# Issuing the 2 MB loads of a rotary-embedding and score kernel as two 1 MB loads each, in consecutive steps

## The chip, the cores and the metric

The kernel runs on one core of a Trainium2 chip. The metric is the device time of one execution, in microseconds, as the median of several; lower is better. A run is timed in turn with runs of the kernel before on the same chip. The trace of one execution of each kernel comes from the hardware profiler. A run counts as "slow", and is left out of ratios, when it is over 1.5% above the fastest of the same kernel.

## The reference

```python
batch, seq, heads, dim = 16, 512, 16, 64            # q, k: float32; cos, sin: [seq, dim / 2]
q1, q2 = q[..., :half_dim], q[..., half_dim:]
q_rot = np.concatenate([q1 * cos_q - q2 * sin_q, q1 * sin_q + q2 * cos_q], axis=-1)
# k_rot in the same way
scores = np.einsum('bshd,bthd->bsht', q_rot, k_rot)  # float32, 268 MB
```

Both inputs are 34 MB each and the output is 268 MB, so four fifths of the bytes are stores.

## The kernel before

The output is made in 64 steps, four for each batch b. A step rotates one quarter ("slot" c) of q and of a later k on DVE, transposes on PE, computes eight pairs of score matrices on PE, copies them from PSUM to a staging buffer on ACT, and stores 4 MB. There are three staging buffers, and two buffers each for q and k. Every transfer of the main loop is issued by SP on one queue, in program order, apart from the "relieved" q loads.

```python
RELIEVED = {("q", 5): 0, ("q", 8): 1, ("q", 11): 2, ("q", 14): 3}
...
def load(which, b):
    t = inb[which][b % 2]
    sem = f"in_{which}{b % 2}"
    rows = [("in", which, b % 2, c) for c in range(C)]
    rest = [("in rest", which, b % 2, c) for c in range(C)]
    if (which, b) not in RELIEVED:
        dma(SP, nc.sync, t.rearrange("p c (h d) -> p c h d", h=H), dram[which][b], sem, writes=rows + rest)
        return
    # relieved: 120 of the 128 partitions are loaded through POOL's queue. A cursor is first moved
    # so that the 15 shares leave out one of the 16 DMA engines (SLOW = 4).
    ...
    plan.add(POOL, None, (), rows)        # POOL waits until the buffer is free
    ...
    halves(0, n, rows, f"part{x}")
...
load("k", 3)
for i in range(C, NST):
    ...                                   # the step; its store is issued when ACT has filled the buffer
    if i % C == C - 2:
        load("q", i // C + 2)
    elif i % C == C - 1:
        load("k", i // C + 3)
```

An engine list ("plan") records what each operation reads and writes and derives every semaphore wait from it, so moving a load can't make a race.

## Time and profile before

| | |
|---|---|
| median of 3 runs | 798.94 us (797.91 to 799.68) |
| PE, ACT, DVE busy | 86%, 71%, 68% of the span |
| 16 DMA engines busy | 99% of the span, 421 GB/s on average |
| transfers | 18,513 packets, 335.87 MB |

The row to look at is the DMA's: every slice but the first and the last is at 9, and PE, busy as it is, waits for ACT, which waits for staging buffers. The lines follow in the prediction.

### The profile page before, as it was taken

The page shows a single profiled execution, that of the slowest core. Times are in us where ns is not written, and L with a number is a line of the kernel's source. Part 1 is how long each engine was busy: PE and PEld are TensorE (multiplying, and loading weights), DVE is VectorE, ACT ScalarE, POOL GpSimd, SP SyncE. Part 2 cuts the span into 40 slices and gives each one's busy share as a digit, 9 for nine tenths or more (in the row PEclk, how much of TensorE's full clock was granted, in tenths as well). Part 3 has the DMA queues.
Part 4 walks back from the last instruction along what each step waited for, and adds up shares of the span by engine and source line. Part 5 has one row for each costly group of instructions (what it writes and reads, how often), then busy time and mean ns, then how long its engine had stood idle before and what let it go on. Part 6 is the DMA issues. An engine that isn't in the chain of part 4 may idle for free.

```text
span 797.1 us, 8197 instructions
## 1 busy us (share of the span) xinstructions
PE 684.3 (86%) x3072; PEld 295.4 (37%) x3072; DVE 545.2 (68%) x516; ACT 562.4 (71%) x647; POOL 8.4 (1%) x18
## 2 busy tenths in 40 slices
PE   3989999897989979799797988979989699789960
PEld 2444443343333434344342433334334244334420
DVE  6999988575775868568585767757758488575400
ACT  3978886785767858578585866768667677678860
POOL 0000000000000000100000000000000100000000
PEclk9999999898998989989898999989989899899995
DMA  8999999999999999999999999999999999999995
GB/s 346 420 424 433 429 418 434 426 434 423 430 413 427 435 434 428 439 421 414 426 427 437 432 435 426 419 428 432 428 431 433 432 429 411 428 432 437 430 433 238
DMA packets 18513, 335.87 MB, mean 421 GB/s; under 512 B 2128, under 2 KB 3408, under 8 KB 4432
## 3 DMA queue, kind: packets, MB, share of 16 engines
q1 hardware_dynamic: 16832, 327.42, 96.5%
q0 software_dynamic: 1376, 8.13, 2.4%
q10 hardware_dynamic: 288, 0.13, 0.1%
q8 instruction: 6, 0.10, 0.0%
q14 instruction: 11, 0.09, 0.0%
HBM read 67.24 MB, written 268.44 MB: 421 GB/s over the span
## 4 chain that ended last, share of the span: by engine, by line
DMA 47%; PE 35%; DVE 8%; ACT 6%; issue 1%; ACTq 0%; DVEq 0%; SPq 0%
DMA out_dram<-st 47%; PE ps L409 27%; PE bank L360 9%; ACT st L418 6%; DVE st L335 3%; DVE part L335 2%; DVE k_sb L335 2%; DVE q_sb L335 1%; DMA st<-in_k_dram 1%; DVE kT L378 0%; DVE qT L378 0%; ACTq L110 0%; DVEq L110 0%; SPq L542 0%; SPq L513 0%
## 5 line engine op out<-in xcount | busy, mean ns | idle before, releaser
L418 ACT COPY st<-ps 128x1024 f32<-128x1024 f32 x512 | 495.5, 1018 | 196.7 <-DMA out_dram<-st 103.3
L409 PE MATMUL ps<-kT,qT 64*128 64x512 f32 x2048 | 542.9, 646 | 71.6 <-ACT st L418 71.6
L409 PEld LDWEIGHTS ps<-kT,qT 64*128 64x128 f32 x2048 | 182.0, 195 | 261.0 <-issue 134.2
L378 DVE COPY qT<-bank 128x512 f32<-128x512 f32 x118 | 81.6, 691 | 197.3 <-PE bank L360 197.3
L360 PEld LDWEIGHTS bank<-ident,q_sb 128*128 128x128 f32 x480 | 54.7, 150 | 101.5 <-issue 99.5
L360 PE MATMUL bank<-ident,q_sb 128*128 128x128 f32 x480 | 85.5, 305 | 1.0 <-DVE q_sb L335 1.0
L360 PEld LDWEIGHTS bank<-ident,k_sb 128*128 128x128 f32 x480 | 50.4, 141 | 94.5 <-DVE k_sb L335 43.1
L360 PE MATMUL bank<-ident,k_sb 128*128 128x128 f32 x480 | 78.6, 287 | 1.6 <-DVE k_sb L335 0.8
L378 ACT COPY kT<-bank 128x512 f32<-128x512 f32 x122 | 72.5, 597 | 6.7 <-PE bank L360 6.7
L335 DVE TENSOR_TENSOR part<-q_sb,ss_t 128x1024 f32<-128x1024 f32 x60 | 73.5, 1225 | 3.2
L335 DVE TENSOR_TENSOR k_sb<-k_sb,part 128x1024 f32<-128x1024 f32 x60 | 73.5, 1225 | 2.1
L335 DVE TENSOR_TENSOR k_sb<-k_sb,cos_t 128x1024 f32<-128x1024 f32 x60 | 73.5, 1225 | 2.0
L335 DVE TENSOR_TENSOR q_sb<-q_sb,cos_t 128x1024 f32<-128x1024 f32 x60 | 73.5, 1225 | 2.1
L335 DVE TENSOR_TENSOR part<-k_sb,ss_t 128x1024 f32<-128x1024 f32 x60 | 73.0, 1216 | 0.3
L335 DVE TENSOR_TENSOR q_sb<-q_sb,part 128x1024 f32<-128x1024 f32 x60 | 72.9, 1216 | 0.0
L360 PE MATMUL bank<-ident,st 128*128 128x128 f32 x64 | 10.8, 319 | 13.2 <-DVE st L335 13.2
L360 PEld LDWEIGHTS bank<-ident,st 128*128 128x128 f32 x64 | 8.2, 161 | 18.5 <-DVE st L335 16.7
L335 DVE TENSOR_TENSOR part<-st,ss_t 128x1024 f32<-128x1024 f32 x8 | 9.8, 1222 | 6.4 <-DMA st<-in_k_dram 6.0
L335 DVE TENSOR_TENSOR st<-st,part 128x512 f32<-128x512 f32 x16 | 11.1, 691 | 0.5
L237 POOL DMA_DIRECT2D scratch<-in_q_dram x6 | 3.6, 600 | 615.4 <-PE bank L360 615.4
L335 DVE TENSOR_TENSOR st<-st,cos_t 128x1024 f32<-128x1024 f32 x8 | 9.8, 1225 | 0.3
L378 ACT COPY qT<-bank 128x512 f32<-128x512 f32 x10 | 5.7, 615 | 3.5 <-PE bank L360 3.5
(11 smaller groups left out, 11.0 us busy)
## 6 DMA issues: line engine op xcount, KB each, us to landing
out_dram<-st SPq DMA_DIRECT2D x60, 4096.0 KB, 25.5
k_sb<-in_k_dram SPq DMA_DIRECT2D x15, 2048.0 KB, 27.1
q_sb<-in_q_dram SPq DMA_DIRECT2D x11, 2048.0 KB, 29.2
out_dram<-st SPq DMA_DIRECT2D x16, 1024.0 KB, 13.3
q_sb<-in_q_dram POOLq DMA_DIRECT2D x4, 1920.0 KB, 32.6
st<-in_k_dram SPq DMA_DIRECT2D x1, 1536.0 KB, 9.0
st<-in_q_dram SPq DMA_DIRECT2D x1, 1536.0 KB, 12.2
st<-in_k_dram SPq DMA_DIRECT2D x1, 512.0 KB, 5.0
```

The lines of the kernel that those rows point to most:

```text
L237: plan.add(engine, one(lambda: e.dma_start(dst, src)), reads, writes, sem=sem, also=also)
L335: plan.add(DVE, one(lambda: nc.vector.tensor_tensor(o, a, b, op=op)), reads, writes, also=more)
L360: done = [nc.tensor.transpose(bank[:, x, :], srcs[x], ident) for x in range(4)]
L378: plan.add(engine, one(lambda: copy(out=dst, in_=src)), [("bank", m)], keys)
L409: nc.tensor.matmul(out=ps[:, r, :], lhsT=lhs[lo:hi, :], rhs=rhs[lo:hi, :], start=True, stop=True)
L418: plan.add(ACT, one(lambda: nc.scalar.copy(out=so, in_=si)), [("ps", y)], [("st", s, p)])
```

## The change

Two 2 MB loads come after two of each four stores, and none after the other two. The change is meant to spread them, 1 MB behind each store, so that the queue always has the same mix.

```diff
-    def load(which, b):
+    def load(which, b, half=None):
...
         if (which, b) not in RELIEVED:
-            dma(SP, nc.sync, t.rearrange("p c (h d) -> p c h d", h=H), dram[which][b], sem, writes=rows + rest)
+            lo, hi = (0, C) if half is None else (half * C // 2, (half + 1) * C // 2)
+            dma(
+                SP, nc.sync, t[:, lo:hi].rearrange("p c (h d) -> p c h d", h=H), dram[which][b][:, lo:hi],
+                sem if half is None else f"{sem}_{half}", writes=rows[lo:hi] + rest[lo:hi],
+            )
             return
...
-    load("k", 3)
+    load("k", 3, 0)
...
-        if i % C == C - 2:
+        if i % C == 0:
+            load("k", i // C + 2, 1)
+        elif i % C == C - 1:
+            load("k", i // C + 3, 0)
+        elif ("q", i // C + 2) not in RELIEVED:
+            load("q", i // C + 2, i % C - 1)
+        elif i % C == C - 2:
             load("q", i // C + 2)
-        elif i % C == C - 1:
-            load("k", i // C + 3)
```

## The prediction

> **What bounds the kernel now.** I read the page's shares of busy time first, then the slices, then the queues, then the chain that ended last, and only then the waits.
>
> The page of the kernel before, busy shares, slices and queues (DMA is the mean busy share of the 16 DMA engines in tenths, GB/s what they moved):
> ```profile
> PE 684.3 (86%) x3072; PEld 295.4 (37%) x3072; DVE 545.2 (68%) x516; ACT 562.4 (71%) x647; POOL 8.4 (1%) x18
> ...
> DMA  8999999999999999999999999999999999999995
> GB/s 346 420 424 433 429 418 434 426 434 423 430 413 427 435 434 428 439 421 414 426 427 437 432 435 426 419 428 432 428 431 433 432 429 411 428 432 437 430 433 238
> DMA packets 18513, 335.87 MB, mean 421 GB/s; under 512 B 2128, under 2 KB 3408, under 8 KB 4432
> ...
> q1 hardware_dynamic: 16832, 327.42, 96.5%
> q0 software_dynamic: 1376, 8.13, 2.4%
> ```
> PE has the most busy time of the computing engines, 86%, and could be taken for the bound. The DMA row says otherwise: every slice is at 9, the first and last excepted, and the queues' shares add to 99%. The stretches of the timeline, split in four, say it with more digits (the columns are the stretch, its length, busy time of PE, PEld, DVE, ACT and POOL, granted clock, DMA share, GB/s):
> ```profile
> 20.00:200.00 180.00, 165.47 (x779) 73.22 (x779) 148.71 (x143) 140.19 (x165) 1.45 (x2) 0.96 1.01 428
> 200.00:400.00 200.00, 178.42 (x788) 75.93 (x786) 139.27 (x131) 143.19 (x164) 2.48 (x4) 0.92 1.00 426
> 400.00:600.00 200.00, 177.15 (x782) 75.02 (x780) 138.37 (x131) 141.53 (x163) 1.33 (x2) 0.93 1.00 429
> 600.00:780.00 180.00, 155.38 (x704) 66.28 (x700) 105.56 (x101) 131.27 (x149) 2.47 (x4) 0.94 1.01 430
> ```
> The DMA share is 1.00 in each. It can pass 1 because two queues interleave on one engine and both packets' times then count. I also counted, from the packet records, how many of the 16 engines have a packet open at each moment: between 15 us after the first packet and the last 10 us there is no 5 us stretch in which 3% of them are idle. There is no hole to fill.
>
> Each of the 64 steps has a 4 MB store (4.194 MB decimal) and on average a quarter of two 2 MB loads (1.049 MB): 5.243 MB, at 428 GB/s 12.25 us. PE needs 684.3/64 = 10.7 us a step and ACT 562.4/64 = 8.8 us. So the transfers set the pace, and 64 times 12.25 us is 784 us; the start and the last stores make the rest.
>
> The chain that ended last, the waits (total us, times, longest) and the issues (KB each, median us from issue to landing) agree:
> ```profile
> DMA 47%; PE 35%; DVE 8%; ACT 6%; issue 1%; ACTq 0%; DVEq 0%; SPq 0%
> ...
> ACT st L418 <- DMA out_dram<-st: 103.3, 30, 7.0
> ...
> SPq L237 <- ACT st L418: 714.1, 76, 16.9
> ...
> out_dram<-st SPq DMA_DIRECT2D x60, 4096.0 KB, 25.5
> k_sb<-in_k_dram SPq DMA_DIRECT2D x15, 2048.0 KB, 27.1
> q_sb<-in_q_dram SPq DMA_DIRECT2D x11, 2048.0 KB, 29.2
> ```
> ACT waits 103.3 us for a store to free a staging buffer: that is the transfers holding back the computing. No line of the waits has DVE waiting for k_sb or q_sb to land, so no load is late. A store lands 25.5 us after its issue though its own 4.194 MB take 9.8 us at 428 GB/s: about 15 us of work lies queued ahead of it. That backlog is why the lumps of two 2 MB loads in four steps leave no hole.
>
> **What the Trainium skill says.** "DMA: Bandwidth & Descriptors", section "Where 436 GB/s comes from", puts the ceiling of the 16 engines at 435 GB/s; the stretches' 426 to 430 are 98 to 99% of that, so the trace agrees that little is left. The same page, "Why small descriptors are slow", gives a fixed overhead of about 3 cycles a packet, so halving a large packet should cost nearly nothing; the packet records here put the fixed part at some 7 ns (below). The same page, "Anatomy of one DMA", fits about 2.0 us of fixed cost to each DMA of the software path, most of it waiting for the last write to be confirmed. This case's SP loads use the hardware path, and on the busy engines the trace shows no such hole between one transfer and the next: packets follow each other directly. And "Rules for kernel authors" asks for at least 1 MiB for each DMA at 128 partitions; the halves are just that.
>
> **The change part by part.**
>
> *What is moved.* k loads from batch 3 on and the q loads from batch 3 on that are not relieved through POOL are split by slot: 13 of k and 9 of q, 22 loads become 44. The order of instructions has 105 rows on SP before and 127 after, which confirms 22; PE, DVE, ACT and POOL have the same rows in the same order. The q half 0 goes one step earlier than the whole did and k half 1 one step later. A k slot of half 1 is first used five steps after its new issue, q half 1 six steps; at 12.25 us a step that is over 60 us against some 27 us to landing. Nothing becomes late.
>
> *What is removed.* No byte. ACT's 103.3 us of waiting will be spread differently, because every step now has 5.24 MB rather than steps of 4.19 and 6.29 MB. As the 16 engines have no hole, this smoothing has nothing to give: 0 us.
>
> *What is added.* A 2 MB load has 128 packets of 16 KB, 8 on each engine. Its two halves have 256 of 8 KB, 16 on each engine, and one more completion write on each. So each engine gets 22 x 8 = 176 packets and 22 completions more. The packet records of before give the medians: 32 KB 1213 ns (7,680 packets), 16 KB 611 ns (3,350), 8 KB 309 ns (3,057, of which 992 are loads of just such half rows through POOL, also 309), 4-byte completions 9 ns. That is linear in the size plus about 7 ns. Two 8 KB packets take 618 where one of 16 KB took 611: 7 ns more. But on one engine a packet starts 3 to 4 ns before the end of the one before, so the true step is 305 or 306 against 607, and the pair costs 3 to 5 ns more. I take both as bounds: 176 x 4 ns = 0.7 us to 176 x 7 ns = 1.2 us. Completions: 22 x (5 to 9 ns) = 0.1 to 0.2 us. **Sum: +0.8 to +1.4 us on each engine**, and because the engines never rest all of it lies on the path that sets the end. SP also issues 22 more transfers of about 1 us, inside the 714.1 us that it waits for ACT: 0 us.
>
> 798.94 + 1.1 = 800.0 us.
>
> **The rivals.**
>
> *Smoothing pays.* If ACT's 103.3 us of waits delayed stores until engines ran dry, even steps would bring some of it back. For it: the 30 waits, up to 7.0 us long. Against it: the DMA share of 1.00 in all four stretches, and the 15 us of backlog. At most it could give what separates 428 from 435 GB/s, 1.6% or 13 us; I expect none of it, as that difference is packets running at their own length.
>
> *Better or worse interleaving.* Some 16 KB packets are stretched: their mean is 635 against the median of 611 ns, in total 24 x 3,350 / 16 = 5.0 us an engine. Most of that is in the four k loads that run beside a relieved q load of POOL (3.2 us), where two queues share an engine and the stretched time is the other queue's data. Splitting moves which packets overlap, not how many bytes do. The remaining 1.8 us could go either way: +/- 1 us.
>
> *Halves cost more than their packets.* If each additional transfer left a hole of 2 us on the busy engines, 22 would add 44 us, to 843 us. Against it: completions here are followed by the next transfer's first packet without a gap. Or rows of 8 KB at a pitch of 16 KB in HBM might be read less evenly; against it, the 992 POOL packets of that shape at 309 ns.
>
> *The slowest engine sets the tail.* In the packet records fifteen engines end within 4.3 us of each other and one ends 3.5 us after the last of these; the relieved loads exist to help it, as one engine's 32 KB packets are mostly 20 to 50 ns longer. If a half load costs that engine more than others, a us or two; the end may also scatter so between executions, as the three times of before scatter over 1.8 us.
>
> **Range and chances.** 800.0 us from the sum. Below, the scatter of before (797.91 to 799.68) and a lucky interleaving allow 797.8; above, the scatter and the tail's engine allow 803.0. Two per cent is 16 us, more than the whole distance to the ceiling, so faster gets 0.01; slower needs the holes of the third rival: 0.02. I chose the middle of +0.8 and +1.4 rather than weighing the two bounds further.
>
> **What would show it.** The packets of the page should rise by 2,816 + 352 to 21,681 at the same 335.87 MB, the share of DMA stay at 1.00 in the stretches, and GB/s fall by less than 1. 8 KB packets should keep 309 ns. ACT's waits for stores should be more in number and shorter, with a similar total, about 100 us; no wait of DVE for q_sb or k_sb should appear. The prediction is wrong if a DMA slice falls below 9 in the middle, if 8 KB load packets take over 330 ns, or if the rate in the stretches passes 432 GB/s.

## The result

The changed kernel took **803.66 us** (four runs, 802.26 to 805.82) against 798.93 us of before. The ratio is 1.0062, with a 95% interval of 1.0037 to 1.0088. A ratio here and below is the mean time of one kernel's fast runs over that of the other's in the same rounds, so not quite the ratio of the medians. That is within 2%, as forecast, but it is 4.7 us, not 1.1 us, and lies above the range, which ended at 803.0.

The page after, slices and queues:
```profile
DMA  9999999999999999999999999999999999999997
GB/s 350 419 424 414 386 436 421 438 424 401 429 429 430 436 428 434 389 436 431 430 431 432 429 432 383 432 432 428 434 433 427 380 438 427 431 432 426 433 431 306
DMA packets 21682, 335.88 MB, mean 420 GB/s; under 512 B 2480, under 2 KB 3760, under 8 KB 4784
...
q1 hardware_dynamic: 20000, 327.43, 96.5%
q0 software_dynamic: 1376, 8.13, 2.8%
```
The packets are as counted ahead (21,681 forecast, 21,682 found). The DMA row is still all 9s but for its end. The GB/s row is not as before: five slices stand at 380 to 401, where before nothing in the middle was under 411. Busy engines moved fewer bytes. Also, q0, POOL's queue, takes 2.8% for the same 8.13 MB in place of 2.4%: its packets took longer.

The four stretches after, columns as in the prediction (the last two are DMA share and GB/s):
```profile
20.00:200.00 180.00, 168.02 (x794) 73.78 (x791) 151.70 (x145) 142.43 (x168) 1.45 (x2) 0.98 1.00 418
200.00:400.00 200.00, 172.16 (x776) 73.11 (x774) 138.59 (x130) 139.72 (x161) 2.48 (x4) 0.95 1.01 427
400.00:600.00 200.00, 177.45 (x782) 74.68 (x784) 137.93 (x130) 143.31 (x165) 1.33 (x2) 0.94 1.01 427
600.00:780.00 180.00, 155.96 (x700) 65.87 (x696) 104.66 (x100) 130.91 (x148) 2.48 (x4) 0.95 1.00 425
```
The first lost 10 GB/s against before, the third 2, the last 5. The waits and issues after:
```profile
ACT st L422 <- DMA out_dram<-st: 124.8, 39, 8.7
...
k_sb<-in_k_dram SPq DMA_DIRECT2D x26, 1024.0 KB, 28.6
q_sb<-in_q_dram SPq DMA_DIRECT2D x18, 1024.0 KB, 27.2
```
ACT's waits for stores were to become more and shorter at the same total. They became more (39 for 30), longer (8.7 us the longest) and larger in total (124.8 for 103.3 us).

**Where the time is.** Two places carry it. The first is the start of the main loop. SP's instructions after, in order of time (start, duration):
```profile
65.11 1.18 SPq L237 DMA_DIRECT2D k_sb<-in_k_dram  x1
76.21 0.33 SPq L237 DMA_DIRECT2D out_dram<-st  x1
```
The half of the first k load goes out at 65.11 us and the next store can only be issued at 76.21 us. A 2 MB load bridged that; a 1 MB load doesn't, and the engines ran dry: the DMA share in the first of the following stretches is 0.81, and by the packet records 1.15 us of all 16 engines went idle. The second place is the four POOL loads. Stretches of the changed kernel at the start and at each of these:
```profile
75.40:77.40 2.00, 2.00 (x14) 0.84 (x10) 1.93 (x3) 2.00 (x3) 0.00 (x0) 1.00 0.81 340
85.40:91.40 6.00, 6.00 (x32) 2.60 (x28) 5.70 (x7) 4.91 (x6) 0.00 (x0) 1.00 1.00 302
187.50:192.50 5.00, 3.20 (x17) 1.30 (x16) 2.01 (x3) 2.40 (x3) 0.00 (x0) 1.00 1.06 341
334.50:339.50 5.00, 3.46 (x18) 1.35 (x16) 2.75 (x3) 2.22 (x3) 0.00 (x0) 1.00 1.06 315
481.50:488.50 7.00, 3.99 (x16) 1.23 (x12) 2.48 (x3) 2.75 (x4) 0.00 (x0) 0.85 0.99 305
630.50:637.50 7.00, 3.38 (x16) 1.39 (x16) 1.92 (x3) 3.24 (x4) 0.00 (x0) 0.93 1.04 314
```
and those of the kernel before, at its start and its second and third POOL load:
```profile
85.40:91.40 6.00, 6.00 (x32) 2.63 (x29) 5.78 (x7) 4.91 (x6) 0.00 (x0) 1.00 0.99 426
...
333.50:338.50 5.00, 2.51 (x14) 0.76 (x10) 1.82 (x2) 0.56 (x2) 0.00 (x0) 1.00 0.99 419
481.50:488.50 7.00, 3.92 (x22) 1.53 (x18) 2.26 (x3) 2.80 (x4) 0.00 (x0) 1.00 1.01 431
```
With the DMA share at 0.99 or more in all but the first, the changed kernel moved 302 to 341 GB/s where the kernel before moved 419 to 431. (GB/s of so short a stretch is rough: the kernel before read 455 at its first POOL load.)

In the packet records it can be seen why the meeting is new. When POOL's load begins, it shares each engine with whatever SP's queue has there. Before, that was stores, and the two went on at 427 to 428 GB/s, averaged over each of the four loads. In the change the second half of the k load of the same batch, issued one step later than the whole load was, is still on its way then: 72, 93, 112 and 104 of its 128 packets were unfinished when the first POOL packet started (0 at all four before). Both loads' packets are stretched there; the 8 KB packets of POOL's queue have a mean of 352 ns in the whole run against 310 ns before, at a median of 309 ns in both.

For the comparisons below I worked out one measure from the packet records. At each moment the rates (bytes by duration) of all open packets are summed; what is missing to 432 GB/s, the rate of undisturbed stores, is lost time of the 16 engines together. "Start" is 67 to 97 us of the span, "POOL" the four POOL loads with 3 us ahead of and 2 us behind each, "behind" the 20 us after that, "rest" the remainder from 97 to 724 us. "Tail" is how long after the median engine the last engine ended its last store. Each row is one trace.

```
kernel                        start  POOL  behind  rest   sum   tail
before                          0.3   1.1    3.8   1.0    6.2    6.4
the change                      3.3   7.8    0.5   0.9   12.4    1.6
halves back to back (e1)        0.2   1.2    2.4   1.6    5.4    6.0
start half only (e12)           2.3   0.9    3.3   0.8    7.3    5.4
POOL halves only (e13)          0.3   2.2    1.9   1.3    5.7    5.6
start and POOL halves (e14)     2.6   7.1    0.2   0.5   10.4    3.0
relieved k whole (e2)           2.8   2.5    2.4   1.9    9.7    8.3
first k whole (e3)              0.3   1.9    5.2   4.7   12.1    7.9
both whole (e4)                 0.5   1.2    2.4   2.0    6.0    7.7
change, POOL waits (e17)        3.0   4.6    0.4   1.2    9.2    2.1
late whole k, no halves (e5)    0.3   3.0    1.3   0.8    5.3    4.2
```
The change lost 3.0 us more at the start and 6.7 us more beside the POOL loads, and 3.3 us less behind them, where the whole k loads of before are stretched: 6.2 us more in all. The packets add their own 1 us or so. Of these the time shows 3.4 us in the profiled runs (spans of 797.1 and 800.5 us), because the tail shrank by 4.8 us: in the kernel before, the last engine ended 6.4 us after the median one, so the median one had that much room. In the change the median engine's last store landed 8.2 us later (807.2 for 799.0 on the trace's clock), the last engine's only 3.3 us later (808.7 for 805.4).

Sum and tail together account for the profiled times: the span less both is 784.5 to 786.7 us in every row. So the table says of each trace whether its engines lost time together or one of them ended late. It doesn't say how either came about.

### The profile page after: what moved, and what is told of

The parts are those of the page before. It is cut to its first block, busy times and chain, and to the rows that moved or that the text cites. A ratio compares the mean times of both kernels' runs of the same rounds, so it can differ in the third digit from the quotient of the medians.

```text
span 800.5 us, 8241 instructions
## 1 busy us (share of the span) xinstructions
PE 680.5 (85%) x3072; PEld 292.0 (36%) x3072; DVE 545.2 (68%) x516; ACT 561.6 (70%) x647; POOL 8.4 (1%) x18
## 2 busy tenths in 40 slices
DMA packets 21682, 335.88 MB, mean 420 GB/s; under 512 B 2480, under 2 KB 3760, under 8 KB 4784
## 3 DMA queue, kind: packets, MB, share of 16 engines
q0 software_dynamic: 1376, 8.13, 2.8%
## 4 chain that ended last, share of the span: by engine, by line
DMA 52%; PE 31%; DVE 8%; ACT 5%; issue 1%; ACTq 0%; DVEq 0%; SPq 0%
DMA out_dram<-st 51%; PE ps L413 24%; PE bank L364 8%; ACT st L422 5%; DVE st L339 3%; DVE part L339 2%; DVE k_sb L339 2%; DVE q_sb L339 1%; DMA sin_t<-in_sin_dram 1%; DVE kT L382 0%; DVE qT L382 0%; ACTq L237 0%; ACT ss_t L459 0%; ACT ss_t L458 0%; ACTq L110 0%
## 5 line engine op out<-in xcount | busy, mean ns | idle before, releaser
L422 ACT COPY st<-ps 128x1024 f32<-128x1024 f32 x512 | 494.6, 1020 | 200.0 <-DMA out_dram<-st 124.8
L413 PEld LDWEIGHTS ps<-kT,qT 64*128 64x128 f32 x2048 | 179.3, 193 | 269.4 <-ACT st L422 139.1
```

The costliest lines, as they stand in the source:

```text
L413: nc.tensor.matmul(out=ps[:, r, :], lhsT=lhs[lo:hi, :], rhs=rhs[lo:hi, :], start=True, stop=True)
L422: plan.add(ACT, one(lambda: nc.scalar.copy(out=so, in_=si)), [("ps", y)], [("st", s, p)])
```

## The experiments

Each kernel was checked for races first, all gave correct results, and each was timed in five rounds (e6 and e7 in three) beside the kernel before on the same chip. The change itself was timed in a session of its own, so it is compared with an experiment through the two ratios to the kernel before.

**My first theory** was that the times of issue do the damage, at the start and at the POOL loads, and not the packets. The rival was the number and size of the transfers.

### e1: the halves, back to back

```diff
     load("k", 3, 0)
+    load("k", 3, 1)
...
-        if i % C == 0:
-            load("k", i // C + 2, 1)
-        elif i % C == C - 1:
+        if i % C == C - 1:
             load("k", i // C + 3, 0)
+            load("k", i // C + 3, 1)
...
+        elif i % C == C - 2 and ("q", i // C + 2) not in RELIEVED:
+            load("q", i // C + 2, 0)
+            load("q", i // C + 2, 1)
```

> The halves are kept (22 more transfers, 2,816 more 8 KB packets) but both halves of a load are issued one after the other at the step of the old whole load. Theory 1, the times of issue do the damage (a k half meets the POOL load of a relieved q, and the thin queue at the start): no collision, so +0 to +1.5 us against before, some 799 to 800.5 us. Rival, the smaller packets and the number of transfers cost it: as slow as the change, 803 to 805 us.

Measured: 800.03 us (798.78 to 801.08) against 798.74, ratio 1.0020 (1.0007 to 1.0033). So 22 transfers and 2,816 packets more cost 1.3 us by medians, 1.6 by the ratio. The rival falls. What sets the change apart from e1 is only the step of issue, and it is worth the difference of the ratios, 0.42% with an interval of some 0.13 to 0.71%: 3.4 us.

### e2, e3, e4: whole loads at the POOL loads, at the start, at both

e2 keeps the k loads of batches 5, 8, 11 and 14 whole at their old step, e3 the first k load, e4 both; everything else is as in the change.

```diff
-        if i % C == 0:
+        if i % C == 0 and ("q", i // C + 2) not in RELIEVED:          # e2
             load("k", i // C + 2, 1)
+        elif i % C == 0:
+            pass
         elif i % C == C - 1:
-            load("k", i // C + 3, 0)
+            load("k", i // C + 3, 0 if ("q", i // C + 3) not in RELIEVED else None)
```
```diff
-    load("k", 3, 0)
+    load("k", 3)                                                       # e3; step 4 then loads no k half
```

> The change, but the k loads of the four batches whose q is relieved (5, 8, 11, 14) stay whole at the old step, so no k half is in flight when a POOL load starts. The four collisions lost some 7.5 us in the trace of the change, and before lost 3.2 us at the whole k loads after each POOL load. Theory 1: 3 to 6 us faster than the change, 797.5 to 800.5 us, and no stretch under 400 GB/s at the POOL loads. Rival (packets and transfers): at most 0.5 us faster than the change, 803 us.

> The change, but the first k load of the main loop (batch 3) whole at its old place. In the trace of the change the engines ran dry for 1.15 us at the start of the main loop and the next half load ran at some 300 GB/s for 5 us, together 3 us. Theory 1, second part: 2 to 3 us faster than the change (800.5 to 802 us) and no idle engines there. Rival: the hole only moves work and the end is as before, 803 to 804 us.

> e2 and e3 together. Theory 1: the two gains add, 5 to 8 us faster than the change, 796 to 799 us, thus at or a little under the kernel before, since the halves of the other loads lose less than whole loads do (in the trace of the change hardware loads without a POOL load beside them lost 2.4 us, in that of before 4.9 us). Rival (packets and transfers): 802 to 804 us.

Measured against 798.74: e2 803.38 us (799.84 to 804.78), ratio 1.0052 (1.0035 to 1.0069); e3 799.65 us in the median of its five fast runs (798.01 to 808.12, and one of 814.22), ratio 1.0033 (0.9995 to 1.0071); e4 801.63 us (798.66 to 804.75), ratio 1.0044 (1.0022 to 1.0067). e2 and e4 are misses: the stretches at the POOL loads did go in both (table), and the start's hole in e4, but the time hardly came back, in e4 by 2 us. Their tails did not shrink as in the change but grew, to 8.3 and 7.7 us. e4's trace lost no more than that of before, but it is of one of its three faster runs (800.91). e3 can't be called: three runs stand at 798 to 800 us and two at 807 and 808. Its trace is of one of these two (806.96). In it the POOL loads lost only 1.9 us, and the rest of the loss lies behind and between them and in the tail.

### e5: no halves, but the four k loads one step later

```diff
-        elif i % C == C - 1:
+        elif i % C == C - 1 and ("q", i // C + 3) not in RELIEVED:     # on the kernel before
             load("k", i // C + 3)
+        elif i % C == 0 and ("q", i // C + 2) in RELIEVED:
+            load("k", i // C + 2)
```

> The kernel before, nothing split; only the k loads of batches 5, 8, 11 and 14 go out one step later, where they should be in flight when the POOL load of the relieved q starts. Theory 1, a load on SP's queue beside a POOL load slows both: stretches near 280 GB/s at each of the four POOL loads, fifteen engines delayed by 2 to 4 us each time, of which the first 5 us or so in all stay hidden behind the one engine that ends 3.5 us after the rest: 803 to 812 us. Rival, the damage comes from smaller transfers: within 1 us of before.

Measured: 796.98 us (796.68 to 798.95) against 799.08, ratio 0.9979 (0.9967 to 0.9992). This is the opposite of what the theory said: a meeting can cost nothing. The table says where the time was saved. The loads did meet (39, 26, 64 and 37 packets, of 128 with 16 KB, were unfinished when POOL's began) and lost 3.0 us in place of 1.1; but behind the POOL loads 1.3 us was lost in place of 3.8, and the tail was 2.2 us shorter. The stretch moved, and got no larger. e5 is also the fastest kernel, by 0.2%.

### e6 and e7: no POOL loads at all

`RELIEVED = {}` in the kernel before (e6), and in the change with the first k load whole (e7).

> The kernel before with no q load relieved through POOL (all loads whole on SP's queue). The slow engine gets 4 x 128 KB more, 4 x 4.85 us; it ended 3.5 to 6.4 us after the others already. If the slow engine sets the end: 815 to 819 us. If its lag is absorbed by the queues: 800 to 803 us. It is the base of the next run.

> The change with no POOL loads and the first k load whole, thus only the halves in consecutive steps. Theory 1 (what costs is the collision with POOL loads and the start, plus 1.3 us of packets): 1 to 2 us slower than e6. Rival, halves in different steps make engines lag more even without POOL loads: 3 us or more slower than e6. Third, even loads help: as fast as e6 or faster.

Measured: e6 807.42 us (803.42 to 808.67), e7 815.66 us (813.84 to 819.68). Without the relief one engine ended 7.6 us after the median engine in e6 and 9.7 us in e7, so the relief is worth 8 us, between my two figures. e7 missed again: with no POOL load to meet, halves in consecutive steps still cost 8 us (e7 against e6). In the traces the measure gives e7 3.1 us more lost than e6 up to 724 us (12.9 for 9.8) and a tail 2.1 us longer, of 5.1 us between the spans. Most of e7's loads from 190 to 470 us are stretched by 1 to 5 us of engine time each, summed over the 16 engines, and single later ones by up to 10. In the change itself all loads but those at the start and at POOL's are stretched by less than 1.2 us each. So e7 may show another regime than the change's own loss; that halves can cost without any POOL load is shown all the same.

### e8, e12, e13, e15, e9: parts of the change alone

All are the kernel before with some loads split in consecutive steps: the nine q loads (e8), the first k load (e12), the k loads of batches 5, 8, 11 and 14 (e13), the other eight k loads (e15), all 13 k loads (e9). The edits are conditions on the batch as in e2.

> Only the q loads (the nine that are not relieved) in two halves in consecutive steps; k loads whole, at the steps of before. No k half is in flight at a POOL load and the start is as before. Theory 1: 9/22 of the packets' cost, +0.5 to +1 us on before, 799.3 to 800 us. Rival, halves in different steps cost by themselves: +2 us or more.

> The kernel before with one load split: the first k load of the main loop (batch 3), its halves in steps 3 and 4. In the change the engines ran dry for 1.15 us there and the next half, read by all 16 engines in step, was stretched by 28.7 us of engine time, 1.8 us an engine: together 2.9 us, on every engine, the slow one included. Theory: 2 to 3.5 us slower than before, 801 to 802.5 us, with idle engines near 78 us of the span. Rival, the start's loss is hidden by later slack: within 0.7 us of before.

> The kernel before with only the k loads of batches 5, 8, 11 and 14 split, the halves in consecutive steps, so that the second half meets the POOL load of the relieved q. In the change these four meetings stretched loads and stores by 108 us of engine time, 6.8 us an engine, in place of 51 us (3.2 us) at the whole k loads behind the POOL loads before. Theory, the slow engine takes no part of the POOL load and sets the end, 6.4 us behind the median engine: the 3.6 us more on the others are hidden, 0 to 1.5 us slower than before. Rival, all of it shows: 3 to 4 us slower, 802 to 803 us.

> The kernel before with the other eight k loads (4, 6, 7, 9, 10, 12, 13, 15) in halves in consecutive steps; no start hole, no k half at a POOL load. Theory, what costs is where a load meets something: +0.3 to +1 us (8/22 of the packets), 798.8 to 800 us. Rival, k halves in consecutive steps make engines drift apart and cost by themselves: +2 us or more, 801 us up.

> All 13 k loads in halves, all q loads whole: the change without its q part. As q halves alone cost nothing, this should lose what the change loses: 802.5 to 804.5 us. Rival, it takes every step loaded alike (k and q halves) for the loss: 799 to 801 us.

```
                       median us (range)            ratio (95% interval)
e8   q halves          798.97 (798.28 to 802.68)    1.0012 (0.9993 to 1.0031)
e12  first k           799.75 (799.00 to 800.69)    1.0015 (1.0002 to 1.0028)
e13  k at POOL loads   797.07 (796.15 to 805.38)    0.9995 (0.9961 to 1.0029)
e15  other k           799.91 (798.88 to 801.19)    1.0010 (0.9997 to 1.0023)
e9   all k, fast runs  799.4  (797.78 to 801.87)    1.0007 (0.9989 to 1.0025)
```
The start's half costs 1.2 us alone; the q halves and the other k halves no more than their packets should; the POOL halves alone nothing, though one of six runs stood at 805.38. Summed they make some 1 to 3 us, not 4.7 (the ratios sum to 1.0032, give or take 0.0043, so the time alone does not settle it), and none of them has the stretches of the change: e13's POOL loads lost 2.2 us, not 7.8. e9 has three more runs at 813 to 814 us, its profile among them. Its four fast runs do not show the loss that I expected, though it has the start's half and all four POOL halves; that speaks against the theory.

### e10 and e11: a fifth relieved load

```diff
-    RELIEVED = {("q", 5): 0, ("q", 8): 1, ("q", 11): 2, ("q", 14): 3}
+    RELIEVED = {("q", 3): 0, ("q", 6): 1, ("q", 9): 2, ("q", 12): 3, ("q", 15): 4}
```

> The kernel before, nothing split, with five relieved q loads (batches 3, 6, 9, 12, 15) instead of four. Each takes 128 KB, 4.85 us, off the slow engine and puts 0.3 us on each other one. Theory, the slow engine alone sets the end of before (it ends 3.5 us after the next): 2 to 4 us faster, 795 to 797 us, the last landing within 3 us of the median one. Rival, the whole set of engines sets the end: 0 to 1.5 us slower.

> The change with five relieved q loads (3, 6, 9, 12, 15). In the change the last landing came only 1.6 us after the median one: fifteen engines, delayed by the meetings with POOL loads, set the end. Theory: no gain, 0 to 3 us slower than the change (803 to 807 us), as a fifth meeting is added. Rival, the slow engine still sets the end: 2 to 4 us faster than the change, 800 to 802 us.

Measured: on the kernel before (e10) 797.52 us, ratio 0.9982 (0.9969 to 0.9994); on the change (e11) 805.70 us (805.27 to 806.02), ratio 1.0086. Taking work off the slowest engine helps the kernel before, by 1 us where 2 to 4 were expected, and does not help the change: 2 us slower by the medians, with intervals of the ratios that overlap. A fifth meeting was not added, as I had expected: in e11's trace the first of its five POOL loads meets no k half. The other four meet 120 to 128 of the 128 packets each, more than in the change, and all five lost 12.2 us in place of 7.8. The signs agree with the tails: in the kernel before one late engine sets the end, in the change nearly all do.

### e14: the start's half and the POOL halves together

The parts didn't sum by their medians, so I formed a second theory: they compound. The hole at the start and the packets make SP's queue late, so that more of the k half is left when POOL's load begins, and each meeting makes it later again.

```diff
-        if i % C == 0 and ("q", i // C + 2) in RELIEVED:                  # e13
+        if i % C == 0 and (i == C or ("q", i // C + 2) in RELIEVED):      # e14, with load("k", 3, 0) ahead of the loop
```

> The kernel before with k loads 3, 5, 8, 11 and 14 in halves in consecutive steps, thus the start (+1.2 us alone) and the POOL meetings (-1.4 us alone) together. Theory, compounding: the start makes the queue late, so more of each k half still waits when the POOL load begins (72 to 112 of its 128 packets in the change, 44 to 81 with the POOL halves alone) and the meetings stretch as in the change: 802 to 804 us, POOL stretches losing 5 us or more. Rival, the two simply add: 798 to 799.5 us.

Measured: 802.85 us (799.20 to 805.24), ratio 1.0042 (1.0020 to 1.0063). Alone the two gave ratios of 1.0015 and 0.9995; together they give two thirds of the whole loss, with 5 of the 22 loads split. In time this is not clear of the noise, as e13's odd run makes the sum of the two uncertain (1.0010, give or take 0.0036); the traces carry the reading. Its stretches at the start and the first three POOL loads:
```profile
85.40:91.40 6.00, 6.00 (x31) 2.45 (x28) 5.77 (x7) 4.91 (x6) 0.00 (x0) 1.00 0.82 269
187.50:192.50 5.00, 2.58 (x14) 0.83 (x12) 1.72 (x2) 2.73 (x4) 0.00 (x0) 1.00 1.01 267
334.50:339.50 5.00, 4.07 (x20) 1.37 (x16) 2.84 (x3) 2.83 (x4) 0.00 (x0) 1.00 1.07 331
481.50:488.50 7.00, 4.02 (x18) 1.42 (x14) 2.98 (x3) 2.78 (x4) 0.00 (x0) 0.84 0.99 316
```
and the same in e13, which has the POOL halves but no hole at the start:
```profile
85.40:91.40 6.00, 6.00 (x32) 2.63 (x28) 5.77 (x7) 4.90 (x6) 0.00 (x0) 1.00 0.98 418
...
187.50:192.50 5.00, 3.84 (x20) 1.41 (x16) 2.89 (x4) 4.30 (x5) 0.00 (x0) 1.00 1.02 398
334.50:339.50 5.00, 3.38 (x10) 1.52 (x12) 0.82 (x2) 3.85 (x4) 0.00 (x0) 0.69 1.06 433
481.50:488.50 7.00, 7.00 (x36) 2.93 (x32) 4.96 (x6) 5.91 (x8) 0.00 (x0) 1.00 1.02 414
```
Packets of the k half unfinished at POOL's first packet were 107, 108, 108 and 92 in e14 against 61, 81, 44 and 66 in e13. The deeper the overlap, the slower both loads: 7.1 us lost against 2.2. e3's trace agrees: all of the change's halves but no hole at the start, 72, 36, 24 and 30 packets unfinished, 1.9 us lost. That the hole makes the overlap deep fits these traces, one of each kernel; e9 contains all of e14's halves and speaks against it in time.

### e17 and e18: POOL's load waits for the k half

The sharpest test leaves every half and its step as in the change and only makes POOL wait until the second k half of the same batch has landed.

```diff
-        plan.add(POOL, None, (), rows)
+        plan.add(POOL, None, [("in", "k", b % 2, 2)], rows)      # e18: with the first k load whole as well
```

> The change with every half at its step; only each POOL load first waits until the second k half of the same batch has landed, some 5 to 8 us later than now. Theory, the meetings are the largest part: POOL stretches lose 2 us or less in place of 7.8, and 2.5 to 4 us of the time come back: 799.5 to 801 us; the start (1.2 us) and the packets (1.3 us) stay. Rival, halves in consecutive steps cost by drift and the meetings only mark where: 802.5 to 804 us as in e2.

> e17 with the first k load whole, so without the start's hole either. Theory: what is left is the packets, 798.8 to 800.3 us. Rival, drift: 801 to 803.5 us, scattered over some us as e3 and e4 were.

Measured: e17 798.42 us (five runs at 797.76 to 799.16, one at 806.39), ratio 1.0018 (0.9987 to 1.0049); e18 798.73 us (796.18 to 804.48), ratio 1.0007 (0.9979 to 1.0036). With that one wait the change is back at the time of the kernel before, as far as the intervals tell: e17's and the change's own, 1.0037 to 1.0088, still overlap, e18's does not. Stretches of e17 at the first two POOL loads, which now begin some 11 us later:
```profile
199.00:204.00 5.00, 2.59 (x12) 1.22 (x12) 2.03 (x3) 1.84 (x3) 0.00 (x0) 0.88 1.08 462
345.50:350.50 5.00, 2.84 (x14) 1.02 (x12) 2.14 (x3) 1.46 (x2) 0.00 (x0) 1.00 1.03 438
```
No stretch there is near 300 GB/s, and no packet of a k load was unfinished at POOL's first. But the measure for POOL still reads 4.6 us, more than the 2 expected: the next k half now meets the last packets of POOL's load at two of the four, and there the rate falls as it did in the change:
```profile
368.00:373.00 5.00, 3.67 (x18) 1.30 (x14) 0.00 (x0) 1.22 (x2) 0.00 (x0) 1.00 1.01 331
662.00:667.00 5.00, 3.12 (x16) 1.11 (x12) 0.00 (x0) 1.01 (x2) 0.00 (x0) 1.00 0.98 308
```
That it nevertheless cost no time was not expected. By the table e17 lost 3.0 us more than the kernel before, and its tail, 4.3 us shorter, made up for it. The start's hole is in e17's trace too (3.0 us), and the median still came out level with before.

### e16: what the runs seemed to point to

e5 with five relieved loads.

> No halves: whole k loads of batches 6, 9, 12 and 15 one step later, and five relieved q loads (3, 6, 9, 12, 15). Late whole k alone gave -0.2%, five reliefs alone -0.2%. If they add: 794.5 to 796.5 us. If both take from the same few us behind the POOL loads: 796.5 to 798 us.

Measured: 799.80 us, ratio 1.0005 (0.9992 to 1.0017). The two gains of 0.2% do not add; the meetings there lost 8.5 us. The version that beats both kernels remains e5, 796.98 us, by 0.2%.

## Why the prediction was wrong

- **The bound** was read rightly. The DMA engines carry the span before and after, and the share stayed near 1.00.
- **The packets** were sized rightly: +0.8 to +1.4 us forecast, 1.3 us by e1's medians and 1.6 us by its ratio.
- **"Better or worse interleaving"** is the term that failed: "Splitting moves which packets overlap, not how many bytes do. The remaining 1.8 us could go either way: +/- 1 us." It took a stretched packet for harmless because the other queue's bytes move meanwhile. That holds for a POOL load beside stores (427 to 428 GB/s) and not for a POOL load beside a load: some 300 GB/s. The term is worth +3.4 us (the change against e1), and e17, which takes the meetings at the start of the POOL loads out, gives back 5 us by the medians and 3.5 us by the ratios.
- **"The four k loads that run beside a relieved q load of POOL"**, on which that term rests, were misread. In the trace of before these loads start 2.4 to 12 us after POOL's last packet, and no packet of POOL's queue is open while they run. So their 3.2 us of stretching was not the other queue's data but lost rate: the measure has 3.8 us lost behind the POOL loads, and one stretch there, 369.4 to 374.4 us, reads 370 GB/s.
- **"Nothing becomes late"** was argued from the consumers alone. It is right for them, as DVE never waits for q_sb or k_sb. But k half 1 issued one step later is late in another sense: it is on the engines when POOL's load begins. I had listed the move and not asked what else starts at that time.
- **"There is no hole to fill"** was true of the kernel before, and carried over to the changed one without leave. The backlog of 15 us is a median; at the start of the main loop it is thin, and halving the load that bridged it opened a hole of 1.15 us, followed by a load at 302 GB/s. Alone that costs 1.2 us (e12).
- **"The slowest engine sets the tail"** was given as a rival with a us or two. It was at work in the other direction: the late engine of the kernel before left 6.4 us in which the delays of the others could hide, and the change used most of it.
- Of what should show it, the packets came out as stated, and the fall in GB/s (up to 10 in a stretch), the mean of 8 KB packets (321 ns on SP's queue, 352 on POOL's) and ACT's waits (longer) were the signs of error.

**What stays open.** Whole k loads at the POOL loads (e2, e4) removed the meetings at least as well as e17 did, yet left 803.4 and 801.6 us, with longer tails; e7 lost 8 us with no POOL load at all. So the meetings are one way in which the time is lost, not the only one. Five kernels with k halves in consecutive steps (e3, e9, e13, e17, e18) have one to three executions 4 to 15 us above their others, which none of the 59 runs of the kernel before had; the rule on slow runs leaves four of these executions out of the ratios, and whether they are the kernel's doing is not known. I take it that the relative phases of the engines decide, but that is argued, not shown. Why two loads slow each other is open too. The order in which POOL's load spreads its rows over the engines is one candidate and the reading of HBM another; no run separates them.

## What to carry to other kernels

On a saturated queue, splitting transfers cost their packets here, which was little (1.3 us for 22), and moved half of each in time, which was more (3.4 us): list every other transfer that starts in the stretch it moves to, above all loads on another queue. A row of busy tenths can stay at 9 while the rate falls by 30% (302 GB/s for 426), so read GB/s beside it. And find out whether one late engine or all of them set the end before pricing a delay that falls on all but one.

## What the Trainium skill lacked or had wrong

- "DMA: Bandwidth & Descriptors", section "Issuing engines are not separate DMA queues": it says that transfers from different issuing engines interleave on the same 16 DMA engines. It lacks that what interleaves matters: a POOL load beside SP's stores went at 427 to 428 GB/s, beside SP's load at 305 to 341 GB/s (the change) and 267 GB/s at worst (e14).
- The same page, section "Latency and other measured facts", calls the slowness of two of the engines specific to the software path, with its cause a guess. The runs show an engine that is late on the hardware path alone: with no load on POOL's queue (e6), one still ended 7.6 us after the median one. Whether it is one of the two that the page means is not shown: the trace does not name engines, and the kernel leaves out the one that it counts as 4 (`SLOW = 4`), where the page has 7 and 15.
- No page has it that a queue's depth at the moment of a change of phase can decide whether a smaller transfer leaves a hole: 1.15 us here, where a 1 MB load stood in for 2 MB ahead of a store issued 11 us later.
